# Two-block transformer kernel: the second block's attentions handed to the scheduler in 32 counted pieces

## The chip, the cores and the metric

The kernel runs on one core of one Trainium2 chip. The time is the device time of one execution in microseconds (us), the median of several executions. Five engines work side by side, each through its own list of instructions in order: TensorE (PE, matrix products and transposes), VectorE (DVE), ScalarE (ACT), GpSimd (POOL) and SyncE (SP, which here only starts transfers). An instruction that waits for a semaphore holds up everything behind it on its engine.

## What is computed

Two blocks of two layers each run one after the other on a sequence of 256 rows of 1024 numbers in float32. The change touches only the mixer of the second block, which is, per layer:

```python
h = rmsnorm_2(x, g_attn[l])
qa, ka, va, qb, kb, vb = jnp.split(h @ w_in[l], offs, axis=-1)
qa = apply_rope_2(rmsnorm_2(qa, qn_a[l]), cos_a, sin_a)      # 8 heads of 64
ka = apply_rope_2(rmsnorm_2(ka, kn_a[l]), cos_a, sin_a)      # 2 heads of 64
ya = windowed_gqa_sink(qa, ka, va, sink[l])
qb, kb = (apply_rope_2(rmsnorm_2(z, g), cos_b, sin_b) ...)   # 4 heads of 2 x 64
lam = exp(sum(lq1 * lk1)) - exp(sum(lq2 * lk2)) + lambda_init
p = softmax(qb @ kb.T * scale)                               # two softmaxes of each head
yb = (p[:, 0] - lam * p[:, 1]) @ vb
yb = rmsnorm_2(yb, subln[l]) * (1.0 - lambda_init)
x = x + concat([ya, yb]) @ w_out[l]
```

A gated feed-forward part with a short convolution follows. The windowed attention has a sink: `exp(sink - m)` joins each row's sum.

## The kernel before, in words

The 256 rows are two tiles t of 128. Every projection is made three times over (`mm3`, L312 to L314): activations and weights are each split in a high and a low part, and high by high, high by low and low by high are added in one PSUM bank. A weight tile of 128x1024 comes by a transfer that SP starts, ACT copies its high part (`wh`, L240) and DVE subtracts to make the low part (`wl`, L228); there are four buffers of each. Every product of a projection is 128 rows by 512 columns (256 for kva).

`layer2` (L1627 on) holds the second block's mixer. Its projections, in the order of the program, are qa (windowed queries, 96 products counting both t), kva (windowed keys and values, 48 narrow ones), then from `w_b2` k, q and v of the differential attention, and `w_out2`. After each projection `qk_rope` (L1600 to L1625) does the norm and the rotation: ACT copies and squares, DVE sums the squares (L1610), POOL adds the epsilon (L1611) and takes the power -0.5 (L1613), and DVE multiplies and adds (all on L228). The tiles are C (qa), A and MG (kva, and k again later); for keys DVE needs POOL's power before it multiplies (`sc is None`), for queries the power goes into the softmax's scale. `turn` transposes the result on PE (L271) through one of the four "mm" PSUM banks that the projections use too, and ACT copies it out (UT holds the windowed queries, K the turned probabilities).

The windowed attention is eight pieces of scores (four head pairs i by two row blocks b, L1685 and L1686). Each piece: DVE takes the maximum (L788), ACT makes two exponentials whose sums it reads out, DVE makes two small additions and a reciprocal (L1696) for the sink, and multiplies the 128x512 probabilities (tiles W, YL, HG). Then PE turns them, multiplies by the values (L1710), and ACT and DVE split the result (OH, OL). The differential attention has eight heads (b, h): scores on PE (L1730), the maximum (L788), two exponentials, a reciprocal (L1735), a small product with lambda, a scaling of the second map (L232) and a multiply-add (L237). `diff_head` of the next head is written ahead of `diff_tail` of this one. Then, per row block, the turned maps meet the values (L1760), the sub-norm runs, and the result (GT) is turned and split (PH, PL) for `w_out2`.

The program's order is made by a scheduler at build time that knows priorities: `urgent()` raises them, and what the program writes first comes first among equals. `defer(key, steps, fn)` holds a piece back until that many matmul steps (`tick`, one for each `mm3`) have passed; `needed` and `all_needed` force pieces out. Before the change the second block's mixer defers nothing of its own: `w_out2` alone, in `proj_resid`, sets `deferring`.

Of the kernel before, what the change touches and what calls it, by code (L numbers as in the profile page):

```python
# [177 lines left out]
def two_block_kernel(tc, a, out):  # L178
# [4 lines left out]
    with ExitStack() as es:  # L183
# [136 lines left out]
        def defer(key, steps, fn):  # L320
            if deferring[0]:
                later.append([key, steps, fn])
            else:
                fn()

        def tick(mm):
            for e in later:
                e[1] -= 1
            while later and later[0][1] <= 0:
                with tc.issue_after(mm.ins), urgent():  # L330
                    later.pop(0)[2]()

        def needed(keys):
            while any(e[0] in keys for e in later):
                with urgent():
                    later.pop(0)[2]()
# [23 lines left out]
        def proj_a(src, nk, n, xx, evac, by_t=False, us=None, ends=False):  # L360
# [3 lines left out]
            if by_t:  # L364
                for t in range(2):
                    gemm_a(us, xx, t, pss[t])
                    if ends:
                        all_needed()
# [287 lines left out]
        def proj_resid(src, xx, nxt, inner=False):  # L656
# [11 lines left out]
            deferring[0] = True  # L668
# [115 lines left out]
        def softmax_rows(ps, p, sc, smax=None):  # L784
# [4 lines left out]
            nb, sums = small(h), small(h)  # L789
# [837 lines left out]
        def layer2(l, norm, nxt_ffn, nxt):  # L1627
# [24 lines left out]
            def turn(gi, h, dst):  # L1652

                for t in range(2):
                    pt = mm_([P, h // 2, P])
                    for i in range(h // 2):
                        tr(pt[:, i, :], late[gi, t][:, i * P : (i + 1) * P])
                    if len(dst.shape) == 3:
                        cp(dst[:, :, t * P : (t + 1) * P], pt)
                    else:  # L1660
                        for e in range(2):
                            k = slice(64 * e, 64 * e + 64)
                            cp(dst[k, :, e, t * P : (t + 1) * P], pt[k])
# [5 lines left out]
            proj_a(a["w_qa2"][l, 0], 2, 512, hx, ev(0, 8, True), by_t=True, ends=True)  # L1669
            proj_a(a["w_kva2"][l, 0], 2, 256, hx, ev_kva)  # L1670
            turn(0, 8, qaT)
            turn(1, 2, kaz)
# [4 lines left out]
            pa = []  # L1677

            def swa_scores(i):

                pa.append(slot(PS[i], [P, 2, 2, 256]))
                for b in range(2):
                    s = ax([P, 2, 256])
                    with pe_order():
                        T.matmul(s, lhsT=qaT[:, i, b * P : (b + 1) * P], rhs=kaz[:, 0], start=True, stop=False)  # L1685
                        T.matmul(  # L1686
                            s[:, :, (1 - b) * P : (2 - b) * P], lhsT=identb, rhs=bm((causal, anti)[b], 2),
                            start=False, stop=True,
                        )
                    p = pa[i][:, b]  # L1690
                    sums, nb = softmax_rows(s, p, fac[0, b].rearrange("p (e i) -> p i e", e=2)[:, i], ns[:, i])
                    es, ri = small(2), small(2)
                    tt(es, nb, ns[:, i], SUB)
                    act(es, es, AF.Exp)
                    tt(ri, sums, es, ADD)
                    V.reciprocal(ri, ri)  # L1696
                    tt(p, p, bc(ri, 256), MUL)

            def swa_out(i):
                pT = pts[:, i % 2].rearrange("p (e k t) -> p e k t", e=2, k=2)  # L1700
                for b in range(2):
# [4 lines left out]
                    cp(pT[:, :, :, b * P : (b + 1) * P], pt)  # L1706
                ot = ax([P, 256])
# [8 lines left out]
            swa_scores(0)  # L1716
            for i in range(4):
                if i < 3:
                    swa_scores(i + 1)
                swa_out(i)  # L1720
            proj_a(a["w_b2"][l, 1], 2, 512, hx, ev(3, 8))
            proj_a(a["w_b2"][l, 0], 2, 512, hx, ev(2, 8))
# [132 lines left out]
```

## Time and profile before

| | us |
|---|---|
| median of three runs | 1715.99 (1715.18 to 1716.37) |
| the profiled execution | 1713.25 |
| its span | 1711.5 |
| PE busy in the span | 1665.4 (97%) |
| DVE busy | 1306.3 (76%) |
| ACT busy | 1019.3 (60%) |
| POOL busy | 127.2 (7%) |

The granted TensorE clock is 1.00 of full speed throughout. The span is the time between the first and the last instruction of the profiled execution; the 1.75 us between it and the execution's time lie around it. The page gives busy shares over the whole program. The second block's mixers lie at 1111 to 1218 us (its first layer) and 1417 to 1521 us (its second), so every question on the change is asked of these two stretches: the timeline of each engine there shows the start and duration of each instruction and, in brackets, how long the engine stood idle before it and whom it waited for.

### The profile page before, as it was taken

The numbers are of one execution on the slowest core, as the hardware profiler recorded it, in microseconds if no ns is written. First come the engines' busy times: TensorE is split into PE (matmuls) and PEld (weight loads), VectorE is DVE, ScalarE is ACT, GpSimd is POOL, SyncE is SP. The second block draws the span as 40 slices with busy tenths as digits, with TensorE's granted clock in tenths as the row PEclk, the third lists the DMA queues.
The fourth block names the chain that finished last, engine by engine and source line by source line (L and its number), as shares of the span: only waits on it lengthen the run. The fifth ranks groups of instructions, "written<-read, shape, count | busy, mean of one in ns | idle before, by whom it ended". The sixth has DMA issues, their size and how long they took to land.

```text
span 1711.5 us, 25116 instructions
## 1 busy us (share of the span) xinstructions
PE 1665.4 (97%) x9081; PEld 1374.5 (80%) x9081; DVE 1306.3 (76%) x2435; ACT 1019.3 (60%) x1789; POOL 127.2 (7%) x186
## 2 busy tenths in 40 slices
PE   8989999999999999999999999999899999999999
PEld 6978778878888888878788888766788886678887
DVE  7979896769966779975666666788777778878776
ACT  5873445557665576354565555667566656766654
POOL 2010100010100100000000000221000012110000
PEclk9999999999999999999999999999999999999999
DMA  6684565646786456456555666553466654346664
GB/s 226 176 279 140 192 189 160 185 150 205 234 267 212 156 163 190 150 157 185 181 162 182 193 188 193 158 156 106 140 195 191 190 171 151 105 140 184 194 187 132
DMA packets 85072, 304.36 MB, mean 178 GB/s; under 512 B 9586, under 2 KB 10098, under 8 KB 84947
## 3 DMA queue, kind: packets, MB, share of 16 engines
q1 hardware_dynamic: 81216, 290.11, 55.4%
q0 software_dynamic: 3440, 12.49, 2.1%
q8 instruction: 71, 1.16, 0.3%
q14 instruction: 55, 0.44, 0.1%
q10 hardware_dynamic: 290, 0.16, 0.0%
HBM read 290.14 MB, written 12.58 MB: 177 GB/s over the span
## 4 chain that ended last, share of the span: by engine, by line
PE 59%; DVE 7%; ACT 4%; issue 2%; POOL 1%; POOLq 0%; ACTq 0%; DVEq 0%
PE ps L426 16%; PE ps L312 10%; PE ps L314 10%; PE ps L313 10%; PE ps L425 7%; PE ps L271 2%; DVE wl L228 2%; ACT wh L240 2%; PE ps L428 1%; PE ps L1730 1%; PE ps L1279 1%; ACT W L240 1%; DVE W L228 1%; DVE xs L228 1%; POOL sm L1613 0%
## 5 line engine op out<-in xcount | busy, mean ns | idle before, releaser
L228 DVE TENSOR_TENSOR wl<-wr,wh 128x1024 fp32r<-128x1024 f32 (+2 forms) x516 | 618.9, 1202 | 174.0 <-ACT wh L240 171.9
L240 ACT ACTIVATE wh<-wr 128x1024 fp32r<-128x1024 f32 (+2 forms) x516 | 536.6, 1042 | 264.4 <-PE ps L314 220.2
L426 PE MATMUL ps<-hh,wh 128*128 128x512 f32 x1280 | 449.9, 396 | 0.1
L425 PE MATMUL ps<-hh,wl 128*128 128x256 f32 x1120 | 312.7, 279 | 1.3 <-DVE wl L228 1.3
L426 PEld LDWEIGHTS ps<-hh,wh 128*128 128x128 f32 x1280 | 234.2, 188 | 46.1 <-PE ps L426 0.4
L312 PE MATMUL ps<-wh,hh 128*128 128x512 f32 (+2 forms) x576 | 222.1, 387 | 3.4 <-ACT UT L240 2.6
L313 PE MATMUL ps<-wl,hh 128*128 128x512 f32 (+2 forms) x576 | 221.9, 386 | 2.5 <-DVE wl L228 2.5
L314 PE MATMUL ps<-wh,hh 128*128 128x512 f32 (+2 forms) x576 | 221.7, 385 | 1.4 <-DVE hh L228 1.4
L425 PEld LDWEIGHTS ps<-hh,wl 128*128 128x128 f32 x1120 | 211.2, 189 | 9.3 <-DVE wl L228 2.3
L313 PEld LDWEIGHTS ps<-wl,hh 128*128 128x128 f32 x576 | 108.4, 188 | 25.6 <-DVE wl L228 5.1
L312 PEld LDWEIGHTS ps<-wh,hh 128*128 128x128 f32 x576 | 108.5, 189 | 24.4 <-ACT UT L240 3.1
L314 PEld LDWEIGHTS ps<-wh,hh 128*128 128x128 f32 x576 | 108.5, 188 | 23.1 <-DVE hh L228 3.0
L312 PE MATMUL ps<-wh,PH 128*128 128x512 f32 x256 | 101.3, 397 | 1.0 <-ACT PH L240 1.0
L313 PE MATMUL ps<-wl,PH 128*128 128x512 f32 x256 | 100.3, 393 | 0.0
L314 PE MATMUL ps<-wh,PL 128*128 128x512 f32 x256 | 100.0, 392 | 0.0
L240 ACT ACTIVATE UT<-ps 128x256 f32<-128x256 f32 (+2 forms) x120 | 47.1, 393 | 61.3 <-PE ps L426 59.3
L312 PE MATMUL ps<-wh,OH 128*128 128x512 f32 x208 | 83.5, 402 | 0.0
L313 PE MATMUL ps<-wl,OH 128*128 128x512 f32 x208 | 83.0, 399 | 0.0
L314 PE MATMUL ps<-wh,OL 128*128 128x512 f32 x208 | 81.5, 393 | 0.0
L240 ACT ACTIVATE MG<-ps 128x256 f32<-128x256 f32 (+1 forms) x84 | 32.0, 381 | 55.8 <-PE ps L426 55.7
L312 PEld LDWEIGHTS ps<-wh,PH 128*128 128x128 f32 x256 | 47.9, 188 | 11.0 <-ACT PH L240 1.7
L313 PEld LDWEIGHTS ps<-wl,PH 128*128 128x128 f32 x256 | 48.1, 188 | 10.2 <-DVE wl L228 0.9
(453 smaller groups left out, 2977.3 us busy)
## 6 DMA issues: line engine op xcount, KB each, us to landing
wr<-in_w_gu SPq DMA_DIRECT2D x160, 512.0 KB, 4.4
wr<-in_w_dn SPq DMA_DIRECT2D x88, 512.0 KB, 3.7
wr<-in_w_gt SPq DMA_DIRECT2D x48, 512.0 KB, 3.7
wr<-in_w_out SPq DMA_DIRECT2D x32, 512.0 KB, 4.0
wr<-in_w_b SPq DMA_DIRECT2D x24, 512.0 KB, 4.2
s5w<-sw SPq DMA_DIRECT2D x16, 704.0 KB, 5.2
wr<-in_w_glu SPq DMA_DIRECT2D x16, 512.0 KB, 3.8
sw<-GT POOLq DMA_DIRECT2D x11, 512.0 KB, 3.9
```

Source lines behind the costliest of these rows:

```text
L228: V.tensor_tensor(out=o, in0=x, in1=y, op=op)
L240: S.activation(out=o, in_=x, func=f, **k)
L271: T.transpose(o, x_, ident[0:k, 0:k])
L312: T.matmul(ps, lhsT=ah, rhs=bh, start=start, stop=False)
L313: T.matmul(ps, lhsT=ah, rhs=bl, start=False, stop=False)
L314: return T.matmul(ps, lhsT=al, rhs=bh, start=False, stop=stop)
L425: T.matmul(ps[:, 0], lhsT=wl_, rhs=xx.hi(kt), start=False, stop=False)
L426: T.matmul(ps, lhsT=wh_, rhs=xx.both[kt], start=first, stop=last)
L428: T.matmul(ps[:, 0], lhsT=wl_, rhs=xx.hi(kt), start=False, stop=False)
L1279: T.matmul(ps[:, a_, :].rearrange("p (n h) -> p n h", h=h), lhsT=kL[:, a_, b * P : (b + 1) * P], rhs=odd(qR[:, a_, b * P : (b + 1) * P], h ...
L1730: T.matmul(s, lhsT=qbT[:, h, b * P : (b + 1) * P], rhs=kbz[:, h], start=True, stop=True)
```

## The change

- `defer` now keeps the held pieces sorted by their remaining steps, and a piece can be held in ordinary priority (`hot=False`); `proj_resid` of the mixer no longer sets `deferring`.
- In the mixer nearly everything is now a held piece with a counted step: eight turns (per projection and t), eight score pieces, four turns and four outputs of the windowed attention, eight differential heads, and a turn, an output and a last turn per row block.
- Turns go through the "ax" banks, one t at a time. The q projection of `w_b2` is made t by t.
- In the windowed softmax the two small additions (16 pairs in the two layers) go from DVE to POOL.
- In the differential attention the two maps are joined unnormalised, p0 - (s0 lambda / s1) p1, so one 128x256 scaling per head falls away; the row sum s0 goes into the sub-norm as EPS s0^2. The head is finished in one function, so no next head is written ahead of it.
- The number of matmuls is the same (9081). DVE has 22 instructions fewer per layer, POOL 16 more.

The core of the diff:

```diff
-            turn(0, 8, qaT)
-            turn(1, 2, kaz)
...
-                    tt(es, nb, ns[:, i], SUB)
-                    act(es, es, AF.Exp)
-                    tt(ri, sums, es, ADD)
+                G.tensor_tensor(out=es, in0=nb, in1=ns[:, i], op=SUB)
+                act(es, es, AF.Exp)
+                G.tensor_tensor(out=ri, in0=sums, in1=es, op=ADD)
...
-            def diff_tail(sums, p):
-                ri, rl = small(2), small(1)
-                V.reciprocal(ri, sums)
-                tt(rl, ri[:, 1:2], nlam, MUL)
-                ts(p[:, 1, :], p[:, 1, :], rl)
-                stt(p[:, 0, :], p[:, 0, :], ri[:, 0:1], p[:, 1, :], MUL, ADD)
...
+                sums = dsum[b][:, 2 * h : 2 * h + 2]
+                softmax_rows(s, p, fac[2, b][:, 2 * h : 2 * h + 2], sums=sums)
+                ri = small(1)
+                V.reciprocal(ri, sums[:, 1:2])
+                stt(ri, ri, nlam, sums[:, 0:1], MUL, MUL)
+                stt(p[:, 0, :], p[:, 1, :], ri, p[:, 0, :], MUL, ADD)
...
+                stt(e4, s0, EPS, s0, MUL, MUL)
...
-                r, r2 = rpow(ss, 4, P), small(4)
-                ts(r2, r, post)
+                stt(ss, ss, 1.0 / P, e4, MUL, ADD)
+                G.tensor_tensor(out=r, in0=ss, in1=nhalf[:, 0:4], op=ALU.pow)
+                ts(r, r, post)
...
+            proj_a(a["w_qa2"][l, 0], 2, 512, hx, ev_turn(0, 8, qaT, (10, 17), True), by_t=True, ends=True)
+            proj_a(a["w_kva2"][l, 0], 2, 256, hx, ev_turn(1, 2, kaz, (6, 6), ev_=ev_kva))
+            for k, st in enumerate((7, 10, 13, 17, 20, 24, 27, 31)):
+                defer(("s", k), st, lambda k=k: swa_scores(k // 2, k % 2), False)
+            for i, st in enumerate((19, 26, 33, 40)):
+                defer(("t", i), st, lambda i=i: swa_turn(i), False)
+                defer(("o", i), st + 3, lambda i=i: swa_out(i), False)
+            for k, st in enumerate((35, 37, 39, 41, 43, 45, 47, 49)):
+                defer(("ds", k), st, lambda k=k: diff_head(k // 4, k % 4), False)
+            for b, st in enumerate(((48, 51, 58), (57, 60, 67))):
+                for k, f in enumerate((diff_turn, diff_out, diff_y)):
+                    defer(("d%d" % k, b), st[k], lambda f=f, b=b: f(b), False)
+            proj_a(a["w_b2"][l, 1], 2, 512, hx, ev_turn(3, 8, kbz, (9, 9)))
+            proj_a(a["w_b2"][l, 0], 2, 512, hx, ev_turn(2, 8, qbT, (9, 9)), by_t=True)
```

What the order becomes is shown at three places, all in the first layer of the second block. Rows name what is written, an arrow, and what is read. First PE at the kva projection (`ps_11281`, `ps_11282` before); C is the rotated windowed query. Before:

```order
L314 MATMUL ps_11282<-wh_11277,hh_10973 128x256
L312 MATMUL ps_11282<-wh_11277,hh_10973 128x256
L313 MATMUL ps_11282<-wl_11279,hh_10973 128x256
L314 MATMUL ps_11282<-wh_11277,hh_10973 128x256
L271 MATMUL ps_11361<-con,C_2160_11208 128x128 x4
L271 MATMUL ps_11367<-con,C_2164_11245 128x128 x4
L312 MATMUL ps_11657<-wh_11635,hh_10973 128x512
```

After:

```order
L312 MATMUL ps_11288<-wh_11265,hh_10973 128x256
L313 MATMUL ps_11288<-wl_11267,hh_10973 128x256
L314 MATMUL ps_11288<-wh_11265,hh_10973 128x256
L312 MATMUL ps_11288<-wh_11265,hh_10973 128x256
L271 MATMUL ps_11295<-con,C_2166_11214 128x128 x4
L313 MATMUL ps_11288<-wl_11267,hh_10973 128x256
L314 MATMUL ps_11288<-wh_11265,hh_10973 128x256
```

The first turn of the windowed queries moved from behind the last kva product to behind the tenth of 48 (in the second layer the seventh).

Second DVE at the rotation of the differential keys (A is the first row tile, MG the second). Before:

```order
L1610 TENSOR_REDUCE sm_11710<-A_2275_11707 128x8
L1696 RECIPROCAL sm_11444<-sm_11444 128x2
L237 SCALAR_TENSOR_TENSOR sm_11458<-sm_11456,sc_2163_11244 128x2
L228 TENSOR_TENSOR W_2210_11428<-W_2210_11428,sm_11444 128x512
L228 TENSOR_TENSOR A_2275_11707<-A_2275_11707,sm_11713 128x512
L1610 TENSOR_REDUCE sm_11724<-MG_2279_11721 128x8
L228 TENSOR_TENSOR A_2275_11707<-A_2275_11707,MG_2126_11102 128x512
L228 TENSOR_TENSOR xs_11717<-A_2275_11707,MG_2126_11102 128x8x32 x2
L228 TENSOR_TENSOR wl_11757<-wr_11753,wh_11755 128x1024
L228 TENSOR_TENSOR A_2275_11707<-A_2275_11707,xs_11717 128x512
L228 TENSOR_TENSOR MG_2279_11721<-MG_2279_11721,sm_11727 128x512
```

After:

```order
L1619 TENSOR_REDUCE sm_11529<-A_2233_11526 128x8
L228 TENSOR_TENSOR A_2233_11526<-A_2233_11526,sm_11532 128x512
L228 TENSOR_TENSOR wl_11576<-wr_11572,wh_11574 128x1024
L228 TENSOR_TENSOR A_2233_11526<-A_2233_11526,MG_2126_11102 128x512
L228 TENSOR_TENSOR xs_11536<-A_2233_11526,MG_2126_11102 128x8x32 x2
L1619 TENSOR_REDUCE sm_11543<-MG_2237_11540 128x8
L228 TENSOR_TENSOR A_2233_11526<-A_2233_11526,xs_11536 128x512
L228 TENSOR_TENSOR MG_2237_11540<-MG_2237_11540,sm_11546 128x512
```

The windowed softmax's work that stood between the sum of A's squares and A's multiplication is gone from there, and the sum of MG's squares moved from right behind that multiplication to behind three more rows, two rows ahead of MG's own multiplication.

Third DVE at the first differential heads (`sm` from `ps` with L788 or L797 is a head's maximum). Before:

```order
L788 TENSOR_REDUCE sm_11943<-ps_11941 128x2
L237 SCALAR_TENSOR_TENSOR sm_11945<-sm_11943,sc_2297_11809 128x2
L788 TENSOR_REDUCE sm_11952<-ps_11950 128x2
L237 SCALAR_TENSOR_TENSOR sm_11954<-sm_11952,sc_2297_11809 128x2
L1735 RECIPROCAL sm_11959<-sm_11946 128x2
L228 TENSOR_TENSOR OL_11382<-ps_11626,OH_11381 128x256
L228 TENSOR_TENSOR sm_11960<-sm_11959,nlam_11114 128x1
L788 TENSOR_REDUCE sm_11967<-ps_11965 128x2
L232 TENSOR_SCALAR W_2323_11937<-W_2323_11937,sm_11960 128x256
L237 SCALAR_TENSOR_TENSOR sm_11969<-sm_11967,sc_2297_11809 128x2
L237 SCALAR_TENSOR_TENSOR W_2323_11937<-W_2323_11937,sm_11959 128x256
```

After:

```order
L797 TENSOR_REDUCE sm_11869<-ps_11867 128x2
L237 SCALAR_TENSOR_TENSOR sm_11871<-sm_11869,sc_2277_11687 128x2
L1743 RECIPROCAL sm_11875<-s5y_11154 128x1
L797 TENSOR_REDUCE sm_11894<-ps_11892 128x2
L237 SCALAR_TENSOR_TENSOR sm_11875<-sm_11875,nlam_11114,s5y_11154 128x1
L237 SCALAR_TENSOR_TENSOR sm_11896<-sm_11894,sc_2277_11687 128x2
L237 SCALAR_TENSOR_TENSOR W_2320_11866<-W_2320_11866,sm_11875 128x256
L228 TENSOR_TENSOR wl_12202<-wr_12198,wh_12200 128x1024
L228 TENSOR_TENSOR wl_12208<-wr_12204,wh_12206 128x1024
L1743 RECIPROCAL sm_11900<-s5y_11154 128x1
```

Before, the second head's maximum and its small product stand ahead of the first head's reciprocal; now the reciprocal, which needs the first head's exponentials, stands ahead of the second head's maximum, and so on for all eight.

## Rows read from the trace of the kernel before

**Rows 1.** Windows of both mixers: us, busy time by engine, clock, DMA share, GB/s.
```profile
1111.00:1218.00 107.00, 98.89 (x488) 71.31 (x487) 85.81 (x213) 71.22 (x171) 21.94 (x23) 1.00 0.38 115
1417.00:1521.00 104.00, 96.85 (x482) 69.91 (x481) 82.33 (x206) 69.34 (x165) 18.88 (x20) 1.00 0.39 117
```

**Rows 2.** PE's timeline at the turns: start, us, instruction, idle before and releaser.
```profile
1111.49 0.39 PE L314 MATMUL ps<-wh,hh 128*128 128x512 f32 x1
1111.72 0.28 PE L312 MATMUL ps<-wh,hh 128*128 128x256 f32 x1
...
1117.50 0.39 PE L313 MATMUL ps<-wl,hh 128*128 128x256 f32 x1 [0.96 <-DVE wl L228]
...
1121.67 0.50 PE L312 MATMUL ps<-wh,hh 128*128 128x512 f32 x1 [1.10 <-ACT UT L240]
...
1125.40 0.33 PE L271 MATMUL ps<-con,A 128*128 128x128 f32 x1 [0.89 <-DVE A L228]
...
1417.22 0.28 PE L312 MATMUL ps<-wh,hh 128*128 128x256 f32 x1
...
1425.93 0.50 PE L312 MATMUL ps<-wh,hh 128*128 128x512 f32 x1 [1.53 <-ACT UT L240]
...
1429.16 0.33 PE L271 MATMUL ps<-con,A 128*128 128x128 f32 x1 [0.90 <-DVE A L228]
```

**Rows 3.** DVE's timeline: the last addition of the first windowed query tile, both layers.
```profile
1114.50 0.68 DVE L228 TENSOR_TENSOR C<-C,xs 128x512 f32<-128x512 f32 x1
...
1417.34 0.69 DVE L228 TENSOR_TENSOR C<-C,xs 128x512 f32<-128x512 f32 x1
```

**Rows 4.** PE's timeline, first layer: a score piece, and the product behind k.
```profile
1136.34 1.02 PE L1685 MATMUL ps<-B,UT 128*128 128x512 f32 x2
...
1140.80 1.08 PE L1710 MATMUL ps<-K,B 128*64 128x256 f32 x8
```

**Rows 5.** DVE's timeline, first layer: key rotation, and the last query rotation's end.
```profile
1141.18 0.69 DVE L1610 TENSOR_REDUCE sm<-A 128x8 f32<-128x512 f32 x1
...
1144.22 0.69 DVE L228 TENSOR_TENSOR A<-A,sm 128x512 f32<-128x512 f32 x1 [1.53 <-POOL sm L1613]
...
1161.59 0.68 DVE L228 TENSOR_TENSOR C<-C,xs 128x512 f32<-128x512 f32 x1
```

**Rows 6.** DVE's timeline: first differential maximum and last multiply-add, both layers.
```profile
1178.85 0.68 DVE L788 TENSOR_REDUCE sm<-ps 128x2 f32<-128x512 f32 x1
...
1185.03 0.34 DVE L232 TENSOR_SCALAR W<-W,sm 128x256 f32<-128x256 f32 x1
...
1198.41 0.48 DVE L237 SCALAR_TENSOR_TENSOR HG<-HG,sm 128x256 f32<-128x256 f32 x1
...
1485.06 0.69 DVE L788 TENSOR_REDUCE sm<-ps 128x2 f32<-128x512 f32 x1 [1.91 <-PE ps L1730]
...
1502.08 0.49 DVE L237 SCALAR_TENSOR_TENSOR HG<-HG,sm 128x256 f32<-128x256 f32 x1
```

**Rows 7.** ACT's timeline among the heads: one exponential, one weight copy.
```profile
1183.83 0.56 ACT L240 ACTIVATE W<-ps,sm,sc 128x256 f32<-128x256 f32 x1 [0.68 <-DVE sm L237]
...
1186.93 1.06 ACT L240 ACTIVATE wh<-wr 128x1024 fp32r<-128x1024 f32 x1 [0.19 <-PE ps L314]
```

**Rows 8.** PE's timeline: output of block 0, and the feed-forward part's first products.
```profile
1201.13 2.02 PE L1760 MATMUL ps<-M,K 128*128 128x128 f32 x16 [1.75 <-DVE GT L228]
...
1217.72 0.40 PE L312 MATMUL ps<-wh,hh 128*128 128x512 f32 x1
...
1521.62 0.39 PE L312 MATMUL ps<-wh,hh 128*128 128x512 f32 x1
```

**Rows 9.** POOL's timeline: a power, and the dearest and cheapest 128x2 addition.
```profile
1113.49 1.98 POOL L1613 TENSOR_TENSOR sc<-sm,nhalf 128x8 f32<-128x8 f32 x1
...
1121.36 1.10 POOL L1611 TENSOR_TENSOR sm<-sm,ne 128x2 f32<-128x2 f32 x1 [1.80 <-DVE sm L1610]
...
1427.61 0.19 POOL L1611 TENSOR_TENSOR sm<-sm,ne 128x2 f32<-128x2 f32 x1 [0.60 <-DVE sm L1610]
```

More of the change, by code (lines that the diff above doesn't have):

```diff
@@ L318, in two_block_kernel, with defer, emit_first @@
         later, deferring = [], [False]
-        def defer(key, steps, fn):
-            if deferring[0]:
-                later.append([key, steps, fn])
+        def defer(key, steps, fn, hot=True):
+            if not deferring[0]:
+                fn()
+                return
+            k = next((i for i, e in enumerate(later) if e[1] > steps), len(later))
+            later.insert(k, [key, steps, fn, hot])
+        def emit_first():
+            _, _, fn, hot = later.pop(0)
+            if hot:
+                with urgent():
+                    fn()
             else:
@@ L366, in proj_a @@
                     gemm_a(us, xx, t, pss[t])
-                    if ends:
+                    if ends and t == 0:
                         all_needed()
@@ L666, in done @@
                 return f
-            deferring[0] = True
+            if not inner:
+                deferring[0] = True
             if inner:
@@ L1650, in ev, with turn, ev_turn, f @@
                 return f
[L1652 to L1663, printed above, removed]
+            def turn(gi, h, dst, t):
+                pt = ax([P, h // 2, P])
+                for i in range(h // 2):
+                    tr(pt[:, i, :], late[gi, t][:, i * P : (i + 1) * P])
+                if len(dst.shape) == 3:
+                    cp(dst[:, :, t * P : (t + 1) * P], pt)
+                else:
+                    for e in range(2):
+                        k = slice(64 * e, 64 * e + 64)
+                        cp(dst[k, :, e, t * P : (t + 1) * P], pt[k])
+            def ev_turn(gi, h, dst, steps, strided=False, ev_=None):
+                def f(t, ps):
+                    (ev_ or ev(gi, h, strided))(t, ps)
+                    deferring[0] = True
+                    defer(("turn", gi, t), steps[t], lambda: turn(gi, h, dst, t), False)
+                return f
             def ev_kva(t, ps):
@@ L1676, in layer2, with swa_scores, swa_turn @@
             ns = nsink.rearrange("p (e i) -> p i e", e=2)
[L1677 to L1692, printed above, removed]
[L1693 to L1699 removed]
+            pa = {}
+            def swa_scores(i, b):
+                if b == 0:
+                    pa[i] = slot(PS[i], [P, 2, 2, 256])
+                s = ax([P, 2, 256])
+                with pe_order():
+                    T.matmul(s, lhsT=qaT[:, i, b * P : (b + 1) * P], rhs=kaz[:, 0], start=True, stop=False)
+                    T.matmul(
+                        s[:, :, (1 - b) * P : (2 - b) * P], lhsT=identb, rhs=bm((causal, anti)[b], 2),
+                        start=False, stop=True,
+                    )
+                p = pa[i][:, b]
+                sums, nb = softmax_rows(s, p, fac[0, b].rearrange("p (e i) -> p i e", e=2)[:, i], ns[:, i])
+                es, ri = small(2), small(2)
+                G.tensor_tensor(out=es, in0=nb, in1=ns[:, i], op=SUB)
+                act(es, es, AF.Exp)
+                G.tensor_tensor(out=ri, in0=sums, in1=es, op=ADD)
+                V.reciprocal(ri, ri)
+                tt(p, p, bc(ri, 256), MUL)
+            def swa_turn(i):
                 pT = pts[:, i % 2].rearrange("p (e k t) -> p e k t", e=2, k=2)
```

62 lines of the change are left out of this document (26 added, 36 removed).

## The prediction

> **What bounds the kernel now.** I read the windows of the two mixers first, since everything the diff touches lies in them. PE is busy 98.89 of 107.00 us in the first and 96.85 of 104.00 in the second, DVE 85.81 and 82.33, ACT about 70, all at full clock [rows 1]. So PE is the bound there as elsewhere, and the change leaves its matmuls as they are. What can be won is the idle PE time, 8.1 + 7.2 = 15.3 us in both layers together; what can be lost has no such limit, because DVE has only some 21 us to spare in each window and its chains end the stage.
>
> Next I read PE's timeline for what it waits on. Around the turns the first layer waits 0.96 on a weight's low part, 1.10 on the copy of the turned queries (the next projection wants a bank of the same four that the turn holds) and 0.89 on the rotated key: 2.95. The second waits 1.53 and 0.90 in the same places: 2.4 [rows 2]. The rest of the idle time stands mostly behind the differential heads: 1.75 ahead of an output product, for the turned result [rows 8].
>
> Last I read DVE and ACT between the turns and the end of the heads, because PE's last work of the mixer (the second half of `w_out2`) can't start until the last head is done. There the time goes from key rotation to query rotation, then windowed pieces at a steady rate, then heads at a steady rate. These rates set the sum.
>
> **The turns.** The old waits fall away, since turns go into other banks and kva is not followed by a bare turn: -2.95 and -2.4. What is late instead is read from the order. The first turn of the windowed queries now stands behind ten kva products. kva starts at 1111.72 and a narrow product takes 0.12 (half the 0.23 from one wide product to the next, 1111.49 to 1111.72 [rows 2]), so PE is there at 1112.9; the last addition of C ends at 1114.50 + 0.68 = 1115.2 [rows 3]. PE waits 2.3, and with it every kva product behind. In the second layer it stands behind seven: 1417.22 + 0.84 = 1418.06, while C ends at 1417.34 + 0.69 = 1418.03, no wait. The key's turn (A) now stands behind 18 products of k; it needs the same DVE work as before, which ends a little later by the wait, so I take 1.15 and 1.1 there, near the 0.89 and 0.90 of before. Sum: 2.3 + 1.15 - 2.95 = +0.5 in the first layer, 1.1 - 2.4 = -1.3 in the second.
>
> **Key rotation and windowed pieces.** From A's turn to the end of k the order of before has 37 products of k, five score pieces and eight probability transposes, from 1125.40 to 1140.80 (the output product behind k starts there [rows 2, 4]). After, it has 30 products and three pieces: 30 x 0.23 + 3 x about 1.0 [rows 4] + 0.7 for the turns = 10.5, from about 1126.0. So k ends at about 1136.5, 4.3 earlier. But then DVE waits for POOL's power. From the sum of A's squares to A's multiplication it takes 1144.22 - 1141.18 = 3.04 [rows 5]. Before, DVE filled all but 1.53 of that with windowed softmax work, and the second tile's wait fully. In the new order nothing stands between sum and multiplication of A: 3.04 - 0.6 = 2.4 idle; for MG only one addition does: 3.04 - 0.6 - 0.6 = 1.8. That is 4.2 idle for 1.5, +2.7. The last query rotation, which ended at 1161.59 + 0.6 = 1162.2 [rows 5], then ends at 1162.2 - 4.3 + 2.7 = 1160.6.
>
> By then fewer windowed pieces are done. Before, five pieces lay between that point and the first differential maximum at 1178.85 [rows 6]: 16.65 / 5 = 3.33 each. After, six are left: 1160.6 + 6 x 3.33 = 1180.6. The two small additions of each piece are now on POOL. That operation's nearest rows are additions of the same size there, 0.19 at the cheapest and 1.10 at the dearest [rows 9]; I take the cheap one with its hand-over, 0.1 more per piece on the chain than on DVE, +0.5. Heads then start at about 1181.1, +2.2, in which the turns' +0.5 is contained. The second layer has the same change of order, with its turns better by 1.8: +0.4.
>
> **The differential heads.** Before, from the first maximum to the last multiply-add takes 1198.41 + 0.48 - 1178.85 = 20.0, in the second layer 1502.08 + 0.49 - 1485.06 = 17.5 [rows 6]. Two heads are in flight: DVE does a maximum, a scaling (0.34 [rows 6]) and a multiply-add for the one while ACT makes exponentials for the other. The change drops the scaling, 8 x 0.3 = 2.4 of DVE work per layer, which lies on that path when DVE is the limit. But it also puts the reciprocal of a head ahead of the next head's maximum. So one head's chain is closed: two exponentials 0.55 apart [rows 7], 1.1; a reciprocal, 0.15; the next maximum, 0.6 to 0.7 [rows 6]; two small products, 0.25; the hand-over to ACT, 0.1. That is 2.2 x 8 + 1.0 at the ends = 18.6. DVE has idle time of its own in each head for weights' low parts. ACT has not: two pairs of weight copies at 1.06 each [rows 7] stand between heads, and each pair holds the next exponentials, less what overlaps the maximum: 2 x 1.75 = 3.5. Together 22.1: +2.1 in the first layer, +4.6 in the second. The bounds: if the copies hide wholly, 18.6 (-1.4 and +1.1); if each pair also waits for PE to give weight buffers back, about 25 (+5 and +7.5).
>
> **The tail.** From the last multiply-add to the first product of the feed-forward part it was 1217.72 - 1198.89 = 18.8 and 1521.62 - 1502.57 = 19.05 [rows 6, 8]. The first row block's turn, output and sub-norm are pieces of their own now and run among the second block's heads, so the 1.75 ahead of an output product [rows 8] should go; the sums are ready earlier as well, and 34 products are left behind the last turn to cover the last norm. I take 17.2: -1.6 and -1.8. Bounds 0 and -2.4. The two additions to the sub-norm are four columns wide and cost next to nothing beside this; the power stays on POOL as before.
>
> **The sum.** First layer 2.2 + 2.1 - 1.6 = +2.7; second 0.4 + 4.6 - 1.8 = +3.2; together +5.9. Against the profiled execution's 1713.25 that is 1719.2; the median of the runs is 2.7 higher than this execution, so 1715.99 + 5.9 = about 1722.
>
> **A rule on the POOL additions.** A DVE operation with two operands in SBUF beside POOL's power shows no lengthening: C's addition at 1114.50 took 0.68 while the power from 1113.49 ran 1.98, and A's multiplication at 1144.22, begun after the power, took 0.69 [rows 3, 5, 9]. So I cost the move to POOL by POOL's own rows and nothing for DVE. The Trainium skill ("SBUF — State Buffer", section "Who interferes with whom") says that DVE's second port pair is shared with GpSimd under an exclusive lock, which speaks against moving additions there: by it each of 16 small additions a layer could wait for, or hold up, a DVE operation of 0.6, an estimate of up to 10 us a layer. The row above does not show it, and the sum goes by the row.
>
> **The rivals.**
> 1. Faster. The pieces fill PE's waits: DVE is lighter by 22 instructions a layer, and if ACT's weight copies hide behind PE, heads take 18.6 (-1.4 and +1.1), the extra windowed piece is paid by DVE time freed (2.2 and 0.4 become -1 and -2), and the tail gives -1.6 and -1.8: together -6.7, 1709. For it: idle PE time of 15.3 to fill [rows 1]. Against: DVE waits seen in the new order at the key rotation and in every head. The Trainium skill ("Perfetto Trace Analysis", section "Optimization Strategy") says that a kernel whose most contended engine changes over time may gain from interleaving those stretches; here PE is the busiest in both windows, with DVE behind it, so the trace bears it out only in part. 0.20.
> 2. Nothing that shows. The rotation's idle time is filled by late work of another kind and the heads' copies half hide, so the stages cost +4 and the tails give -3.4: about 1716.5. 0.25.
> 3. The forecast, closed head chain and idle rotation, slower by 3.4 to 11: 1722. 0.47.
> 4. Much slower: POOL's small additions cost their dear 1.10 [rows 9] in each piece that lies on the chain, 2 x 0.9 x 6 = 11 a layer at most, of which half is hidden: +5.5 a layer more, 1733. It decides from about 0.4 per addition. 0.08.
>
> That the pieces don't stand where the counts put them is visible already: some turns of k and q land later than their steps, since a priority and a free bank decide too; it is part of 3.
>
> **How the numbers follow.** About 0.2%, 3.4 us, is what a measurement of this kernel can tell from no change. Faster by more (below 1712.6): rival 1, 0.20. Within: 0.25. Slower (above 1719.4): 3 and 4, 0.55. The range goes from 1710 (heads at 18.6, tails full) to 1730 (heads at 25 in one layer and near it in the other, no dear POOL): it leaves out rival 4 and somewhat over half of rival 1's chance.
>
> **What would show it.** In the changed kernel's trace: PE waits about 2.3 ahead of C's first turn in the first layer and not in the second; DVE idles about 2.4 and 1.8 at the two key multiplications; the differential maximum comes every 2.2 to 2.5 us, with ACT's exponentials never overlapping two heads; the last multiply-add is 4 to 5 later against the start of the mixer in both layers; from there to the feed-forward part about 17. I am wrong if the maxima come every 1.7 with copies hidden, or if DVE's waits at the rotation cost nothing because the windowed pieces are not what ends the stage.

## The result

The changed kernel takes 1731.68 us (median of four runs, 1729.24 to 1733.1); the kernel before took 1715.59 beside it. The ratio is 1.0096, 95% interval 1.0084 to 1.0108: 16 us slower. The forecast was 1722, range 1710 to 1730: the direction was right, the size was not. The profiled execution of the changed kernel has a span of 1730.9 for 1711.5, so its trace holds the whole loss. (The list under the change makes 38 held pieces in each layer, not the 32 of the title.)

The windows of both mixers, as in [rows 1], each now taken to the end of its longer mixer. The columns are busy time by engine, granted clock, DMA share and GB/s.

```profile
1111.00:1228.00 117.00, 103.25 (x491) 75.06 (x489) 82.08 (x191) 72.97 (x173) 32.10 (x40) 0.96 0.34 107
1427.00:1541.00 114.00, 103.81 (x486) 76.07 (x484) 78.87 (x184) 70.28 (x168) 31.83 (x38) 0.93 0.34 107
```

Each mixer is ten microseconds longer. DVE is busy for less time than before, PE idles 13.8 and 10.2 us, and the granted clock is no longer 1.00. A few marks say in which stage the time went. In the timelines of PE (first fence) and DVE (second), these are kva's start and the first product of the feed-forward part in each layer, and the first maximum and last multiply-add of the differential heads.

```profile
1112.39 0.28 PE L312 MATMUL ps<-wh,hh 128*128 128x256 f32 x1
...
1227.73 0.39 PE L312 MATMUL ps<-wh,hh 128*128 128x512 f32 x1
...
1427.22 0.28 PE L312 MATMUL ps<-wh,hh 128*128 128x256 f32 x1
...
1540.73 0.39 PE L312 MATMUL ps<-wh,hh 128*128 128x512 f32 x1
```

```profile
1182.39 0.68 DVE L797 TENSOR_REDUCE sm<-ps 128x2 f32<-128x512 f32 x1
...
1205.20 0.48 DVE L237 SCALAR_TENSOR_TENSOR HG<-HG,sm 128x256 f32<-128x256 f32 x1
...
1494.89 0.68 DVE L797 TENSOR_REDUCE sm<-ps 128x2 f32<-128x512 f32 x1
...
1517.70 0.48 DVE L237 SCALAR_TENSOR_TENSOR HG<-HG,sm 128x256 f32<-128x256 f32 x1
```

Against [rows 2, 6, 8], with what was forecast. The first layer counts from the program's start (0.7 of its 3.5 stood ahead of kva already, 1112.39 for 1111.72), the second from its own kva:

| stage | first layer | second layer | forecast |
|---|---|---|---|
| up to the first maximum | 1182.4 for 1178.85: +3.5 | 67.7 for 67.8: -0.2 | +2.2, +0.4 |
| heads, first maximum to last multiply-add | 23.3 for 20.0: +3.3 | 23.3 for 17.5: +5.8 | +2.1, +4.6 |
| tail, to the feed-forward part | 22.05 for 18.8: +3.2 | 22.55 for 19.05: +3.5 | -1.6, -1.8 |
| sum | +10.0 | +9.1 | +2.7, +3.2 |

So 10.1 of the 13.2 us by which the forecast fell short stand in the tail, 2.4 in the heads, under 1 ahead of them.

**The head chain is closed, as forecast.** DVE's timeline at the heads of the first layer:

```profile
1184.53 0.16 DVE L1743 RECIPROCAL sm<-s5y 128x1 f32<-128x1 f32 x1 [1.27 <-ACT W L240]
1184.62 0.67 DVE L797 TENSOR_REDUCE sm<-ps 128x2 f32<-128x512 f32 x1
...
1188.32 0.67 DVE L797 TENSOR_REDUCE sm<-ps 128x2 f32<-128x512 f32 x1
...
1190.54 0.67 DVE L797 TENSOR_REDUCE sm<-ps 128x2 f32<-128x512 f32 x1
...
1195.22 0.67 DVE L797 TENSOR_REDUCE sm<-ps 128x2 f32<-128x512 f32 x1
...
1200.33 0.67 DVE L797 TENSOR_REDUCE sm<-ps 128x2 f32<-128x512 f32 x1
```

The maxima come every 2.2 to 2.4, and 3.7 and 5.1 apart where a pair of weight copies stands between; DVE waits ahead of the reciprocal for ACT in six of the eight heads, 0.8 to 1.3 each time.

**Then PE runs dry.** PE's timeline, and the windows of 5 us around it:

```profile
1199.49 1.71 PE L1739 MATMUL ps<-Q,A 128*128 128x512 f32 x2 [1.69 <-ACT YL L240]
...
1202.55 3.79 PE L1762 MATMUL ps<-M,K 128*128 128x128 f32 x16 [0.16 <-ACT HG L240]
...
1209.99 1.93 PE L1762 MATMUL ps<-M,K 128*128 128x128 f32 x8 [2.97 <-DVE GT L228]
...
```

```profile
1190.00:1195.00 5.00, 5.00 (x22) 2.94 (x20) 3.11 (x11) 3.48 (x12) 0.00 (x0) 1.00 0.36 114
1195.00:1200.00 5.00, 3.31 (x16) 2.04 (x16) 3.42 (x7) 4.29 (x10) 0.00 (x0) 0.99 0.00 0
1200.00:1205.00 5.00, 4.35 (x15) 2.74 (x14) 3.30 (x14) 2.99 (x9) 1.80 (x1) 0.50 0.68 210
1205.00:1210.00 5.00, 2.03 (x12) 1.81 (x10) 1.86 (x7) 1.63 (x9) 1.01 (x1) 0.83 0.00 0
1210.00:1215.00 5.00, 5.00 (x25) 4.83 (x26) 1.26 (x2) 1.41 (x8) 0.00 (x0) 0.66 0.00 0
```

Three things are to be seen here. The output products of the first row block come at 1202.55, behind the last score on PE, which waits 1.69 for ACT: only 3.1 ahead of the end of the last multiply-add. The granted clock is 0.50 in the window after PE first stands idle, the lower of its two levels (1.2 for 2.4 GHz), and those sixteen products take 3.79, where [rows 8] has 2.02. And the second block's products wait 2.97 for the first block's sub-norm, because their PSUM bank is the one that it reads: the four "ax" banks are handed out in turn, and in the order of the pieces the second output takes the fourth after the first. In the second layer this wait is 2.81.

### The profile page after: what moved, and what is told of

Its sections match the earlier page's. It is cut to its first block, busy times and chain, and to the rows that moved or that the text cites. A ratio compares the mean times of both kernels' runs of the same rounds, so it can differ in the third digit from the quotient of the medians.

```text
span 1730.9 us, 25118 instructions
## 1 busy us (share of the span) xinstructions
PE 1676.8 (97%) x9081; PEld 1384.4 (80%) x9081; DVE 1298.3 (75%) x2391; ACT 1020.4 (59%) x1789; POOL 149.3 (9%) x218
## 4 chain that ended last, share of the span: by engine, by line
PE 57%; DVE 7%; ACT 5%; POOL 3%; issue 2%; DMA 1%; POOLq 0%; ACTq 0%; DVEq 0%
PE ps L434 15%; PE ps L313 9%; PE ps L314 9%; PE ps L312 9%; PE ps L433 7%; PE ps L271 2%; DVE wl L228 2%; ACT wh L240 2%; POOL sm L1620 1%; PE ps L436 1%; PE ps L1762 1%; PE ps L1739 1%; PE ps L1288 1%; DVE W L228 1%; ACT W L240 1%
## 5 line engine op out<-in xcount | busy, mean ns | idle before, releaser
L314 PEld LDWEIGHTS ps<-wh,PL 128*128 128x128 f32 x256 | 48.1, 188 | 9.7
```

What stands on the lines that cost most here:

```text
L314: return T.matmul(ps, lhsT=al, rhs=bh, start=False, stop=stop)
```

## The experiments

The theory after the comparison: the closed chain of the heads makes them longer, lets PE run dry and so the clock fall; the bank adds a wait of its own in the tail. The rivals: the additions on POOL delay the windowed attention; the turns' places cost the time; the tail is the bank alone. Ratios are to the kernel before, measured beside each (1715.6 beside the changed kernel, 1714.4 to 1714.8 beside the experiments), with 95% intervals.

| kernel | median us | ratio |
|---|---|---|
| changed kernel | 1731.7 | 1.0096 (1.0084 to 1.0108) |
| e1, heads two in flight | 1717.7 | 1.0017 (1.0008 to 1.0027) |
| e2, small additions on DVE | 1737.4 | 1.0131 (1.0116 to 1.0146) |
| e3, kernel before with the new algebra | 1711.8 | 0.9984 (0.9974 to 0.9993) |
| e4, another bank | 1729.2 | 1.0088 (1.0068 to 1.0108) |
| e5, e1 and e4 | 1712.8 | 0.9990 (0.9980 to 0.9999) |
| e6, e5 with later turns | 1713.2 | 0.9993 (0.9984 to 1.0002) |
| e7, e3 with additions on POOL | 1717.9 | 1.0017 (1.0008 to 1.0027) |
| e8, epsilon of the queries on DVE | 1736.2 | 1.0129 (1.0114 to 1.0144) |
| e9, e3 with the bank freed | 1709.8 | 0.9966 (0.9954 to 0.9979) |
| e10, kernel before with the bank freed | 1712.5 | 0.9985 (0.9976 to 0.9994) |
| e11, e3 with closed heads | 1729.9 | 1.0086 (1.0071 to 1.0101) |
| e12, e9 with turns in the other banks | 1721.7 | 1.0042 (1.0028 to 1.0055) |

**The heads: e1, and e11 from the other side.** e1 gives the changed kernel its two heads in flight back:

```diff
+                cur.append((sums, p))
+                if len(cur) > 1:
+                    diff_tail(*cur.pop(0))
+                if b == 1 and h == 3:
+                    diff_tail(*cur.pop(0))
+
+            cur = []
+
+            def diff_tail(sums, p):
                 ri = small(1)
                 V.reciprocal(ri, sums[:, 1:2])
...
```

> The changed kernel with one edit: a differential head's reciprocal, small product and multiply-add are emitted after the next head's maximum and exponentials, as in the kernel before. Closed-chain theory (the head chain of 2.2 to 2.4 us costs what the heads lose, the tail is a loss of its own): the maxima come 1.7 to 1.9 apart where no weight copy stands between, 2 to 4 us less per layer, 1724 to 1728, the tail from the last multiply-add to the feed-forward part stays near 22. Clock theory (the closed chain lets PE run dry, the granted clock falls, and the tail is long because of that): heads 2 to 4 less and the tail back to about 19 in each layer, 1718 to 1722. Bank theory (the tail is long because the second row block's output waits for a PSUM bank): as the first.

It came out at 1717.7, fourteen less, just under the lowest of its ranges. In DVE's timeline of e1 the maxima of the first layer now stand like this, with the last multiply-add; PE's first product of the feed-forward part follows, and one window of the tail:

```profile
1182.36 0.68 DVE L797 TENSOR_REDUCE sm<-ps 128x2 f32<-128x512 f32 x1
1183.15 0.68 DVE L797 TENSOR_REDUCE sm<-ps 128x2 f32<-128x512 f32 x1
1184.59 0.67 DVE L797 TENSOR_REDUCE sm<-ps 128x2 f32<-128x512 f32 x1
...
1196.35 0.69 DVE L797 TENSOR_REDUCE sm<-ps 128x2 f32<-128x512 f32 x1
...
1199.27 0.48 DVE L237 SCALAR_TENSOR_TENSOR HG<-HG,sm 128x256 f32<-128x256 f32 x1
```

```profile
1220.27 0.39 PE L312 MATMUL ps<-wh,hh 128*128 128x512 f32 x1
```

```profile
1200.00:1205.00 5.00, 2.97 (x21) 2.33 (x20) 3.88 (x7) 3.05 (x9) 1.01 (x1) 1.00 0.08 31
```

They start where they did and the eighth comes 6.3 earlier (1196.35 for 1202.61), though not at the even pace of 1.7 to 1.9 that I expected. The heads take 17.4 in each layer, 5.9 less than closed, where every theory had 2 to 4; the tail is 20.5 in each, 1.5 and 2.0 less, and the windows of 5 us through both tails show a clock of 1.00. So the loss is more than the heads' own 5.9: the theory of the clock had the sign of the rest, and a tail of 19 that was not reached.

e11 does the one part alone, in the kernel before with the new algebra:

```diff
-                    cur = diff_head(b, h)
-                    if prev:
-                        diff_tail(*prev)
-                    prev = cur
-            diff_tail(*prev)
+                    diff_tail(*diff_head(b, h))
```

> e3 with the differential heads closed: each head's reciprocal, small product and multiply-add written right behind its exponentials, ahead of the next head; nothing else of the change's order. If the closed chain alone makes the loss, 5 to 8 us more per layer than e3, 1721 to 1727, with PE running dry among the heads and a lower granted clock in the tail. If it costs only in the counted order of the change, where fewer products are left beside the heads, 1712 to 1716.

1729.9 for e3's 1711.8, 18 us and more than the 1721 to 1727 expected. With no piece deferred, no addition moved and no turn shifted, this edit alone makes as large a loss as the whole change. Windows of 5 us of e11, first layer:

```profile
1195.00:1200.00 5.00, 2.25 (x11) 1.62 (x11) 4.12 (x12) 3.11 (x8) 0.00 (x0) 0.81 0.60 143
1200.00:1205.00 5.00, 2.61 (x17) 2.38 (x15) 1.60 (x9) 2.64 (x13) 1.01 (x1) 0.84 0.16 67
1205.00:1210.00 5.00, 4.23 (x20) 4.26 (x21) 1.98 (x3) 0.60 (x1) 0.00 (x0) 0.50 0.00 0
```

PE idles and the clock falls here too, and 3.16 us of wait stand ahead of the second output. In its profile the loss lies in the heads themselves: they take 24.0 and 23.6 for e3's 16.5 and 15.2, the tails 21.9 and 21.5 for 20.0 and 21.8.

**The bank: e4 and e5, e9 and e10.** In e4 two steps are exchanged, so that the second output is handed out ahead of the first block's last turn and gets another bank; e5 joins it with e1.

```diff
-            for b, st in enumerate(((48, 51, 58), (57, 60, 67))):
+            for b, st in enumerate(((48, 51, 60), (57, 58, 67))):
```

> The changed kernel with two steps exchanged: the second row block's output (step 58) stands before the first block's last turn (60), so that it gets another PSUM bank than the first block's output. Bank theory: the 2.97 and 2.81 us that the second output waits ahead of its products go, and both sub-norms overlap; 2.5 to 5 less per layer, 1722 to 1727. Clock theory: the wait only moves, the tail stays within 1 us, 1730 to 1732.

> The changed kernel with the edits of e1 and e4 together: two heads in flight, and the second row block's output ahead of the first block's last turn. If the tail's wait for a PSUM bank is a cost of its own, the tail falls from e1's 20.5 to 18 or 18.5 in each layer and the time to 1712 to 1715. If e4's gain was only a part of what e1 already gives back (a clock that stays up), the tail stays near 20 and the time at 1717 to 1718.

e4's median is 2.5 lower, between the two theories' ranges, and its interval contains that of the changed kernel, so by the times alone a gain is not shown; e5 gained 4.9 over e1. e4's four executions fall in two pairs: 1726.8 and 1727.1 with a mean granted clock of 0.996 and 0.997, 1731.2 and 1731.7 with 0.993 and 0.991. The profile is of the first pair. Windows, first layer and then second, and PE's output products:

```profile
1200.00:1205.00 5.00, 3.86 (x11) 2.06 (x12) 4.03 (x12) 2.72 (x9) 1.80 (x1) 0.59 0.55 199
1205.00:1210.00 5.00, 4.31 (x26) 4.08 (x26) 1.20 (x7) 2.44 (x13) 1.01 (x1) 0.73 0.03 11
1515.00:1520.00 5.00, 3.61 (x28) 2.99 (x27) 2.77 (x10) 3.32 (x18) 1.01 (x1) 1.00 0.04 15
```

```profile
1203.53 3.78 PE L1762 MATMUL ps<-M,K 128*128 128x128 f32 x16 [0.15 <-ACT HG L240]
1207.53 1.15 PE L1762 MATMUL ps<-M,K 128*128 128x128 f32 x8
...
1513.83 2.05 PE L1762 MATMUL ps<-M,K 128*128 128x128 f32 x16 [0.41 <-ACT HG L240]
1516.05 1.16 PE L1762 MATMUL ps<-M,K 128*128 128x128 f32 x8
```

The wait for the bank is gone in both layers. Both layers run the same order, but in this execution the first had the low clock and the second had 1.00: the tail is 19.9 in the first and 18.15 in the second. That prices the clock at 1.7 in one tail, and the sixteen products of the first output alone, 3.78 for 2.05, make up that difference. e5 has tails of 18.1 and 18.2, both at a clock of 1.00; on DVE and PE, first layer:

```profile
1199.04 0.48 DVE L237 SCALAR_TENSOR_TENSOR HG<-HG,sm 128x256 f32<-128x256 f32 x1
```

```profile
1217.62 0.39 PE L312 MATMUL ps<-wh,hh 128*128 128x512 f32 x1
```

The tail of 22 is thus 18.1, plus about 2.4 for the bank (e1's 20.5 less 18.1; at the low clock, the first layer's 22.05 less e4's 19.9 gives 2.15), plus the rest of 1.5 to 2.0, which e4's 1.7 puts down to the clock.

e10 and e9 free that bank in the kernel before, by writing the two last turns behind both outputs; e9 has the new algebra as well.

```diff
...
-                trans_split(y.rearrange("p h e -> p (h e)"), 4, ybh, ybl, 0, b)
+                oo.append(y)
+            for b, y in enumerate(oo):
+                trans_split(y.rearrange("p h e -> p (h e)"), 4, ybh, ybl, 0, b)
```

> The kernel before with the change's algebra (as e3) and the two last turns written behind both outputs, so that the second output doesn't need the bank of the first. In e5 the tail came down to 18.1 in both layers where that bank was free. If the same holds here, the tails of e3 (20.0 and 21.8) come to 18 to 18.5, 4 to 5 us less in all, 1706 to 1709. If the tail of e3 is set by the end of the windowed part's products or the last norm, 1711 to 1712.

> The kernel before with only the two last turns behind both outputs, maps normalised as before. Its tails are 18.8 and 19.05; if the bank holds them up too, to 18 to 18.5, 1713 to 1715; if not, 1715.

Both gained against the kernel before: e10 1712.5, e9 1709.8, the fastest of all and 0.34% under the kernel before (interval 0.21% to 0.46%). But e10's profile has tails of 20.1 and 18.5, so there the gain is not where it was expected; its profiled execution was no faster than that of before, and where the 2 us of the median went is not settled. e9's profile has 18.9 and 20.9 for e3's 20.0 and 21.8: a microsecond each, short of the 18 to 18.5 expected, as far as one execution of either tells. Two more stand ahead of the heads of the second layer (68.35 from its kva for 70.34), so e9's gain over e3, 2.0 by medians with intervals that overlap, is not shown to be the bank's.

**The algebra: e3.** The kernel before with the maps joined unnormalised and the sums in the sub-norm, heads as they were.

```diff
-                V.reciprocal(ri, sums)
-                tt(rl, ri[:, 1:2], nlam, MUL)
-                ts(p[:, 1, :], p[:, 1, :], rl)
-                stt(p[:, 0, :], p[:, 0, :], ri[:, 0:1], p[:, 1, :], MUL, ADD)
+                V.reciprocal(ri, sums[:, 1:2])
+                stt(ri, ri, nlam, sums[:, 0:1], MUL, MUL)
+                stt(p[:, 0, :], p[:, 1, :], ri, p[:, 0, :], MUL, ADD)
...
```

> The kernel before with only the algebra of the change: maps joined unnormalised, row sums into the sub-norm, heads still two in flight, nothing deferred. If DVE sets the pace of the heads before (1.65 to 1.7 us from maximum to maximum), 0.3 less per head, 2.4 per layer, 1711 to 1713. If ACT's exponentials and weight copies set it, no change, 1715 to 1716.

1711.8, as the first theory had it: the heads fell from 20.0 and 17.5 to 16.5 and 15.2, by 3.5 and 2.3 for the 2.4 of the scalings. The tails of its profile gave 3.9 of these 5.8 back (20.0 and 21.8 for 18.8 and 19.05), and the stretch ahead of the second layer's heads another 2.5 (70.34 from kva for 67.84), so that the profiled execution, the slowest of its ten, is no faster than that of before (1713.8 for 1713.25). By medians this part of the change is a gain of 2.8 us, hidden under the rest; where it lies is not shown.

**POOL: e2, e7 and e8.** e2 takes the windowed softmax's two small additions back to DVE in the changed kernel; e7 puts them on POOL in e3; e8 puts the epsilon addition of the query rotations on DVE in the changed kernel.

```diff
-                G.tensor_tensor(out=es, in0=nb, in1=ns[:, i], op=SUB)
+                tt(es, nb, ns[:, i], SUB)
...
-                G.tensor_tensor(out=ri, in0=sums, in1=es, op=ADD)
+                tt(ri, sums, es, ADD)
```

```diff
-            G.tensor_tensor(out=ss, in0=ss, in1=add.to_broadcast([P, h]), op=ADD)
+            (G if sc is None else V).tensor_tensor(out=ss, in0=ss, in1=add.to_broadcast([P, h]), op=ADD)
```

> The changed kernel with one edit: the windowed softmax's two small additions back on DVE. POOL theory (POOL's addition of 6.73 us at 1151 and the pieces queued behind it delay the windowed attention, and so all that follows): 2 to 4 us less per layer, 1724 to 1728. The others: 16 DVE additions of 0.1 us per layer more, hand-overs less, within 1 us of the changed kernel.

> The kernel before with the change's algebra (as e3) and its move of the windowed softmax's two small additions to POOL, nothing deferred. In the changed kernel the move is worth about 4 us a layer (e2 without it). If that is because DVE, in order, no longer waits there for ACT's exponentials, it holds here too: 3 to 8 us less than e3, 1704 to 1709. If it belongs to the changed order alone, 1711 to 1712.5, and more where POOL is held up by DVE's runs.

> The changed kernel with the epsilon addition of the query rotations on DVE, not POOL. If POOL's addition of 6.73 us (beside an unbroken run of two-operand DVE work) is on the path, 2 to 3 us less per layer, 1725 to 1728. If it only looks so in the chain of waits, because DVE and ACT have other work until then, within 1.5 us of the changed kernel; the power behind it may then take the long time in its place.

None came out at a time that its theories gave. e2 is 6 us slower than the changed kernel: from kva on, the heads start 3.8 and 3.3 later in its layers. So in that order POOL's additions are a gain. e7 is 6 us slower than e3: in the order of before the same move is a loss, which only the half sentence on a held-up POOL had left room for. In all three the scheduler also put other DVE instructions of the windowed pieces into another order, so these times are those of an edit with the order that it brings, and not of POOL alone. What the traces do show is how POOL works beside DVE. POOL's timeline of the changed kernel, first layer, and DVE's where the long addition ends:

```profile
1151.14 6.73 POOL L1620 TENSOR_TENSOR sm<-sm,ne 128x8 f32<-128x8 f32 x1 [4.27 <-DVE sm L1619]
...
1159.55 1.86 POOL L1620 TENSOR_TENSOR sm<-sm,ne 128x8 f32<-128x8 f32 x1
```

```profile
1156.60 1.22 DVE L228 TENSOR_TENSOR wl<-wr,wh 128x1024 fp32r<-128x1024 f32 x1
1157.73 0.68 DVE L1619 TENSOR_REDUCE sm<-C 128x8 f32<-128x512 f32 x1
```

An addition of 128x8 that takes 0.20 at the cheapest, and between 1.05 and 2.39 in four other places of these two mixers, took 6.73, beside a run of DVE multiplications, additions and weight subtractions without a pause; it ended 0.14 after the run gave way to a reduction, which has one operand. The second layer repeats the duration to the hundredth. In e8, where that addition is gone from POOL, the powers behind it take the time:

```profile
1152.36 11.45 POOL L1622 TENSOR_TENSOR sc<-sm,nhalf 128x8 f32<-128x8 f32 x2 [4.67 <-DVE sm L1620]
```

Two powers take 3.3 to 4.8 otherwise in the changed kernel. The Trainium skill ("SBUF — State Buffer", section "Who interferes with whom") names an exclusive lock on the ports that DVE and GpSimd share; these rows agree with it, though no run here took the lock away, so that it is the cause is not shown. From kva on, e8's heads start 1.9 and 1.8 later than the changed kernel's in its two layers. But the longer hold is not what delays them. DVE's next windowed multiplication behind it stands here in the changed kernel (first fence) and in e8 (second), whose kva starts 0.51 later:

```profile
1164.79 0.69 DVE L228 TENSOR_TENSOR W<-W,sm 128x512 f32<-128x512 f32 x1
```

```profile
1164.87 0.69 DVE L228 TENSOR_TENSOR W<-W,sm 128x512 f32<-128x512 f32 x1
...
1168.05 1.23 DVE L228 TENSOR_TENSOR wl<-wr,wh 128x1024 fp32r<-128x1024 f32 x1 [2.42 <-ACT wh L240]
```

Up to there e8 has lost nothing against the changed kernel. Its loss lies behind, where DVE's order is another one and DVE waits 2.42 for a weight copy; what of that order costs the time stays open, and so does whether the hold of 6.73 costs any.

**The turns: e6 and e12.** e6 is e5 with the windowed queries turned at steps 17 and 20, not 10 and 17; e12 is e9 with the turns in the attentions' banks.

```diff
-ev_turn(0, 8, qaT, (10, 17), True)
+ev_turn(0, 8, qaT, (17, 20), True)
```

```diff
-                    pt = mm_([P, h // 2, P])
+                    pt = ax([P, h // 2, P])
```

> e5 with the turns of the windowed queries seven and three steps later (17 and 20 for 10 and 17). If the 2.26 us that PE waits ahead of that turn in the first layer delays all that follows, 2 us less than e5 in the first layer, none in the second: 1710 to 1713. If the windowed pieces are paced by DVE anyway, the heads start as before and nothing changes against e5.

> e9 with one more piece of the change: the turns of the rotated queries and keys go through the banks of the attentions, not those of the projections (no piece deferred, not split by t). If the waits of the projections for a bank that a turn holds (1.10 in the first layer, 1.53 in the second, before) are time on the path, 1 to 2.5 us less than e9, 1707.5 to 1709. If DVE's chain through the rotations and the windowed pieces sets the start of the heads, as e6 suggests, the heads start as in e9 and the time stays within 0.7 us of it; the changed order of the pieces can cost some.

e6 is e5 again, 1713.2 for 1712.8, with the wait ahead of the first turn gone: the first maximum stands at 1182.25 for 1182.14. In the second layer, where that wait was nothing, the heads start 1.6 later from kva on. On PE's timeline of e6 the next wait has taken its place, 2.28 for the 1.25 that it is in e5:

```profile
1126.82 0.33 PE L271 MATMUL ps<-con,A 128*128 128x128 f32 x1 [2.28 <-DVE A L228]
```

e12 lost 12 us against e9, where its expectations had 0.7 at most and the changed order as a cost without a number. The 1.06 that e9 waits for a bank is gone, but the wait for the rotated key behind it grew from 0.93 to 2.02: again DVE is what is late. The larger part lies later: the first maximum comes 9.5 behind that of e9, of which 1.7 stood ahead of the mixer. With other banks the scheduler places the windowed pieces and the turns in another order; which of them costs the time stays open.

## Why the prediction was wrong

**The turns: right in size, of no effect.** PE waits 2.26 ahead of the first turn of the queries in the first layer (forecast 2.3) and not in the second, and 1.20 ahead of the key's (forecast 1.15); the second layer's 1.1 is 0.18 there and 1.17 at the key's second tile. PE's timeline:

```profile
1116.00 0.63 PE L271 MATMUL ps<-con,C 128*128 128x128 f32 x4 [2.26 <-DVE C L228]
...
1126.95 0.33 PE L271 MATMUL ps<-con,A 128*128 128x128 f32 x1 [1.20 <-DVE A L228]
```

But e6 takes the first away and gains nothing, so the term should have been nought in the first layer's sum: there DVE, not the turn, sets when the heads start.

**The key rotation: right.** DVE idles 2.03 and 1.80 at the two multiplications (forecast 2.4 and 1.8), and the last query rotation ends at 1161.3 (forecast 1160.6, with the mixer starting 0.7 later):

```profile
1140.82 0.69 DVE L228 TENSOR_TENSOR A<-A,sm 128x512 f32<-128x512 f32 x1 [2.03 <-POOL sm L1622]
...
1146.91 0.69 DVE L228 TENSOR_TENSOR MG<-MG,sm 128x512 f32<-128x512 f32 x1 [1.80 <-POOL sm L1622]
...
1160.66 0.68 DVE L228 TENSOR_TENSOR C<-C,xs 128x512 f32<-128x512 f32 x1
```

The first maximum, forecast at 1181.1, came at 1182.4.

**The heads: right mechanism, a little short.** 22.1 was forecast, 23.3 came: the two gaps with ACT's pairs of copies are 1.4 and 2.8 over the pace of 2.3, 4.2 for the 3.5 I took. Set against the heads of before this was a term of +6.7 in both layers together; e1 shows that closing the chain costs 5.9 in each layer against the open chain with the same algebra. I had the algebra's gain inside the term, and so never saw how dear the one edit is.

**The tail: the step that failed.** I took 17.2, less than before, for two reasons that the trace denies. The first is a row that I misread. The 1.75 of [rows 8] stands ahead of the second row block's output, not of block 0's, and it is no wait for a turned result: PE and DVE of the kernel before show the first output and the sub-norm's read of its bank, which ends at 1200.99, just ahead of the second output at 1201.13.

```profile
1194.61 1.95 PE L1760 MATMUL ps<-M,K 128*128 128x128 f32 x16
```

```profile
1200.30 0.69 DVE L228 TENSOR_TENSOR GT<-ps,sm 128x512 f32<-128x512 f32 x1
```

So the wait for the bank was in my rows already. I let it vanish; it grew to 2.97 and 2.81, and e4 and e5 take it away with the bank. The second reason is that I wrote that the first row block's output and sub-norm "run among the second block's heads". In the kernel before that output began 4.3 ahead of the end of the heads; now it begins 3.1 ahead, at 1202.55, though ACT had copied its turned maps by 1196.5: it stands behind the last score on PE, which waits for ACT, and PE keeps its order. Even with two heads in flight (e1) it is 2.9. (All three are of the first layer.) Further I took the tail's durations from rows at full clock, although my own heads left PE without work. The tail came to 22.05 and 22.55: the 17.2 is short by 0.9 where the bank is free and the clock full (e5's 18.1), by about 2.4 for the bank and by 1.5 to 2.0 for the clock. The bounds I gave, 0 to -2.4, had no room for a loss at all.

**The rivals.** The faster one needed the copies to hide behind PE; the opposite happened. The dear POOL additions (1733 would have been near the time) were not the cause: the windowed pieces' own additions take 0.20, but for one of 0.88 in each layer, and e2 without them is slower still.

**The row on DVE and POOL** that I set against the Trainium skill's rule showed only that DVE is not lengthened. The other side, POOL held up, stood in [rows 9] already: 1.10 for an addition that takes 0.19.

## What to carry to other kernels

When a function that finished an item one step late is written as one piece, look in each in-order engine's list for the item's last step ahead of the next item's first: a chain closed like this cost 6 to 8 us per layer over eight items, and more in the stage that it starved. Price a loss of overlap to its end: where a longer chain leaves PE without work, the stage behind it may run at the lower clock, as in both layers of the changed kernel and of e11 and in one of e4, and neither the durations nor the waits of the old trace hold there. Ask of a wait that is to vanish what it waits for: whoever ended it may only have given back a bank. And separate the parts of a change: here the algebra (e3) with a freed bank (e9) is 0.34% faster than before, under a reordering that lost 1%.

## What the runs showed of the hardware

A POOL addition of 128x8 was held for 6.73 us, and two powers took 11.45, beside an unbroken run of DVE operations with two operands in SBUF; the addition ended 0.14 after a reduction began on DVE, the first of the powers 1.6 after one, about the 1.64 that a power takes at the cheapest. The longer hold delayed DVE's next windowed multiplication no more than the shorter (e8). The granted clock fell to 0.50 in both tails of the changed kernel, after PE had idled 1.7 and 2.9 of 5 us, and stood at 1.00 through the tails of e1, where PE idles 2.0 and 1.7 of 5 us in two windows running. The same order of instructions (e4) had 0.59 in one layer and 1.00 in the other of one execution, so the order alone does not decide it, and what does stays open. The changed kernel's executions spread accordingly, from 1729.2 at a mean clock of 0.994 to 1733.1 at 0.991.
